# A hybrid transformer block on one core: filler matmuls at stage boundaries, weight tiles in rounds of two, and attention work moved

## The chip, the core and the metric

The kernel runs on one core of a Trainium2 chip. The core's engines have queues of their own and meet only at semaphores: TensorE (PE; its weight loads are shown as PEld), VectorE (DVE), ScalarE (ACT), GpSimd (POOL, hardly used here) and SyncE (SP), which issues the DMAs. The metric is the device time of one execution in microseconds (us).

## The reference

One layer: a half-step SwiGLU feed-forward layer, attention, and a second half-step feed-forward layer, on 256 tokens of 2048 features, in float32.

```python
f = swiglu(modulate(rms_norm(h, g_ffn1[l]), sh1, sc1), w1_gate[l], w1_up[l], w1_down[l])
h = h + 0.5 * gt1[:, None, :] * f
nrm = modulate(rms_norm(h, g_mix[l]), sh2, sc2)
q, k, v = jnp.split(nrm @ w_qkv[l], 3, axis=-1)      # 16 heads of 128
...
o_na = rms_norm(o_na.reshape(B, S, D_NA), g_out_na[l])     # heads 0 to 7
o_dil = rms_norm(o_dil.reshape(B, S, D_DIL), g_out_dil[l]) # heads 8 to 15
mix = jnp.concatenate([o_na, o_dil], axis=-1) @ w_o[l]
h = h + gt2[:, None, :] * mix
f = swiglu(modulate(rms_norm(h, g_ffn2[l]), sh3, sc3), w2_gate[l], w2_up[l], w2_down[l])
h = h + 0.5 * gt3[:, None, :] * f
```

The nine vectors `sh`, `sc` and `gt` come from `silu(c) @ w_ada + b_ada`, a product of one vector with a matrix of 2048 by 18432.

## The kernel before

Features lie on the partitions and the 256 tokens on the columns. All weights are streamed once, in tiles `rw` of 128 x 1024 (512 KB, eight blocks of 128 x 128). For precision each tile is split: ACT rounds it to `hiw` (L146), DVE subtracts to get the rest, `low` (L149). The activations are split in the same way and lie side by side, so that a block takes two matmuls: `hiw` times both halves (512 columns) and `low` times the upper half (256 columns). `hiw` and `low` have four buffers each, `rw` has five. Class `W` hands the tiles out in order: `prepare` issues and splits ahead, up to three tiles beyond the one in use (`AHEAD`); `add` collects eight blocks and then runs the eight `hiw` matmuls (L353) and the eight `low` matmuls (L355).

The adaLN vectors are 144 columns. Each is one DMA of 1 MB and one dot product of 2048 elements on DVE (L129), called a dot below. They are queued with `bg_add` and spread by a rate (`pace`): so many dots per weight tile. `bg_until` forces the rest at a point.

The program runs through these stages:

- the start: squares, the first norm, and six k-steps of the first layer done with unsplit weights (L514), each needing two dots;
- the first feed-forward layer: up (`pa`, `pb`), down (`pd`); its tiles are `w1_a` to `w1_e`;
- attention: 96 units of one tile project queries, keys and values in four groups of four heads (three times eight units a group, L637 and L640); 32 units of one tile are the output projection (`wo_unit`, L674 and L679), first over heads 0 to 7 (`b` = 0, units 96 to 111), then over heads 8 to 15 (`b` = 1, units 112 to 127). Between the units stand the steps of the heads, at units that `PLAN` and `PLAN_L` give as (a, b, c, d): transposes `pT`, scores, transposes `pP` of the softmax, and the product `po`;
- the second feed-forward layer, likewise, with tiles `w2_a` to `w2_e`.

At the end of a stage comes a norm over features. `Stat` squares each finished `h`, adds the squares on DVE (`sqa`), and sums them over the partitions with two matmuls with a matrix of ones (`pstat`, L208 and L209); `rstd_from` (L164) turns the sum into `rsr` with two ACT and four DVE instructions. Then `norm_pair` (L222, L223, L225) makes the next stage's `nx` two at a time; the first eight tiles of the next stage run while the later pairs are made.

The output norm of the attention is applied after the projection: `fin` (L654) copies the upper half of `pso` (ACT), adds the lower half, multiplies by the gate and the row `rsr`, and adds to `h` (DVE). So it waits for the sum over all eight heads of its half.

Order: tile dependencies are tracked by a framework that also orders each engine's queue. Where `manual_schedule` is open, or an instruction is pinned with `keep_in_program_order`, the order is that of the code: PE alone in units 8 to 120, PE, DVE and ACT (`BORDER`) from the last quarter of the first layer's down projection to unit 7, and again from unit 121 (`END - TAIL`) to the end of the second layer's first eight tiles. Elsewhere the framework chooses.

Of the kernel before, what the change touches and what calls it, by code (L numbers as in the profile page):

```python
# [9 lines left out]
F32 = mybir.dt.float32  # L10
# [27 lines left out]
PLAN_L = ((4, 6, 9, 11), (6, 8, 11, 13), (7, 9, 12, 14), (9, 11, 14, 15))  # L38
# [5 lines left out]
RQ = 0.35  # L44
# [3 lines left out]
WARM = 8  # L48
ARA = 2
# [17 lines left out]
def build(tc, a):  # L67
    nc = tc.nc
    with ExitStack() as ctx:
# [17 lines left out]
        def bank(nm):  # L87
            return pools["p"].tile([P, 512], F32, tag="b", name=nm)

# [86 lines left out]
        class Stat:  # L176
# [11 lines left out]
            def add(self, t, last_dve=True, late=False):  # L188
# [13 lines left out]
                elif n < total:  # L202
                    self.late = sq
                    if not late:
                        self.fold()
                else:
# [92 lines left out]
        class W:  # L299
            def __init__(self):  # L300
# [6 lines left out]
                self.credit = 0.0  # L307

# [9 lines left out]
            def prepare(self, ahead=AHEAD, pin=False):  # L318
# [11 lines left out]
            def chunk(self):  # L330
                self.prepare()
                self.tail += 1
                return self.ready.pop(self.tail - 1)

            def add(self, out, r, first, last, then=None, whole=False):
# [3 lines left out]
                self.todo.append((out, r, first, last, whole))  # L339
# [7 lines left out]
                for b, (out, r, first, last, whole) in enumerate(todo):  # L347
                    w = hi[:, b * P : (b + 1) * P]
                    if whole:
                        nc.tensor.matmul(out[:, :S], w, r[:, 0, :], start=first, stop=False)  # L350
                        nc.tensor.matmul(out[:, :S], w, r[:, 1, :], start=False, stop=False)
                    else:
                        nc.tensor.matmul(out, w, r, start=first, stop=False)  # L353
                for b, (out, r, first, last, whole) in enumerate(todo):
                    nc.tensor.matmul(out[:, :S], lo[:, b * P : (b + 1) * P], r[:, 0, :], start=False, stop=last)  # L355
# [22 lines left out]
        def up_mm(ps, k0, k1, first, last, then=None):  # L378
            for j in range(2):
                for k in range(k0, k1):  # L380
                    end = k == k1 - 1
                    ws.add(ps[:, j, :], nx[k], first and k == k0, last and end, then if end and j else None)
# [17 lines left out]
        def ffn_down(fs, hid, gate, stat=None, out=None, order=None):  # L400
            acc_ = {}
            for d, f in down_order(fs):
# [4 lines left out]
                if order is not None and d == KT - 4 and f == fs[0]:  # L407
                    order.enter_context(tc.manual_schedule(engines=BORDER))
# [3 lines left out]
                def update(d=d, whole=whole):  # L412
# [5 lines left out]
                    if stat is not None:  # L418
                        stat.add(h[d], late=d >= KT - 4)
# [518 lines left out]
```

## Time and profile before

| | |
|---|---|
| time, median of 3 (lowest to highest) | 1939.87 us (1939.45 to 1940.7) |
| the profiled execution | 1940.85 us |
| its span, first to last instruction | 1939.0 us |
| busy: PE, DVE, ACT | 1900.1, 1524.3, 902.8 us |
[...]
| moved by DMA | 503.98 MB, 260 GB/s |

Busy is the time in which an engine had at least one instruction under way. Matmuls overlap, so PE busy for 98% of the span says that PE rarely stood still, not that it ran at its best rate. Around the span lie 1.85 us of the execution in which no instruction is shown.

### The profile page before, as it was taken

The numbers are of one execution on the slowest core, as the hardware profiler recorded it, in microseconds if no ns is written. First come the engines' busy times: TensorE is split into PE (matmuls) and PEld (weight loads), VectorE is DVE, ScalarE is ACT, GpSimd is POOL, SyncE is SP. The second block draws the span as 40 slices with busy tenths as digits, with TensorE's granted clock in tenths as the row PEclk, the third lists the DMA queues.
The fourth block names the chain that finished last, engine by engine and source line by source line (L and its number), as shares of the span: only waits on it lengthen the run. The fifth ranks groups of instructions, "written<-read, shape, count | busy, mean of one in ns | idle before, by whom it ended". The sixth has DMA issues, their size and how long they took to land.

```text
span 1939.0 us, 27422 instructions
## 1 busy us (share of the span) xinstructions
PE 1900.1 (98%) x10528; PEld 1653.7 (85%) x10528; DVE 1524.3 (79%) x2058; ACT 902.8 (47%) x1327; POOL 0.7 (0%) x6
## 2 busy tenths in 40 slices
PE   8999999999999998999999997999999999999999
PEld 6888888888888887888788886888888888888888
DVE  7999999999788888799977897668865655545665
ACT  2545444433344454555555654544444433334442
POOL 0000000000000000000000000000000000000000
PEclk9999999999999999999999998999999999999999
DMA  9998888889988888589854453669866556656664
GB/s 400 404 362 310 312 309 302 312 330 408 343 308 341 314 312 292 199 329 323 321 192 163 153 157 105 198 213 321 321 206 186 189 189 187 193 187 188 190 194 134
DMA packets 120084, 503.98 MB, mean 260 GB/s; under 512 B 13329, under 2 KB 15633, under 8 KB 101521
## 3 DMA queue, kind: packets, MB, share of 16 engines
q1 hardware_dynamic: 119952, 502.24, 73.8%
q8 instruction: 82, 1.34, 0.3%
q14 instruction: 50, 0.40, 0.1%
HBM read 500.09 MB, written 2.10 MB: 259 GB/s over the span
## 4 chain that ended last, share of the span: by engine, by line
PE 90%; DVE 5%; DMA 2%; issue 1%; ACT 1%; SPq 0%; ACTq 0%; DVEq 0%
PE pb L353 29%; PE pd L353 16%; PE pb L355 15%; PE pd L355 8%; PE pqv L637 3%; PE pqk L637 3%; PE pqq L637 3%; PE pa L353 3%; PE pa L514 2%; DVE low L149 2%; PE pqv L640 2%; DMA ra<-in_w_ada_dram 2%; PE pa L355 1%; PE pqk L640 1%; PE pqq L640 1%
## 5 line engine op out<-in xcount | busy, mean ns | idle before, releaser
L146 ACT CAST hiw<-rw 128x1024 fp32r<-128x1024 f32 x644 | 674.0, 1050 | 784.5 <-PE pd L353 228.8
L149 DVE TENSOR_TENSOR low<-rw,hiw 128x1024 fp32r<-128x1024 f32 x644 | 782.7, 1221 | 302.7 <-ACT hiw L146 300.0
L353 PE MATMUL pb<-nx,hiw 128*128 128x512 f32 x2432 | 610.7, 393 | 4.1 <-DVE nx L225 4.1
L353 PEld LDWEIGHTS pb<-nx,hiw 128*128 128x128 f32 x2432 | 438.5, 189 | 83.3 <-issue 4.8
L355 PEld LDWEIGHTS pb<-nx,low 128*128 128x128 f32 x2432 | 332.3, 191 | 24.8 <-DVE low L149 1.2
L353 PE MATMUL pd<-hd,hiw 128*128 128x512 f32 x1384 | 346.7, 392 | 0.0
L355 PE MATMUL pb<-nx,low 128*128 128x256 f32 x2432 | 339.9, 283 | 0.5 <-DVE low L149 0.5
L353 PEld LDWEIGHTS pd<-hd,hiw 128*128 128x128 f32 x1384 | 248.9, 189 | 44.4
L129 DVE CUSTOM_DVE_ANT_0 ra<-ra,cb,vec 128x2048 f32<-128x2048 f32 x109 | 255.6, 2345 | 15.7 <-DMA ra<-in_w_ada_dram 15.3
L355 PEld LDWEIGHTS pd<-hd,low 128*128 128x128 f32 x1408 | 191.8, 190 | 14.0 <-DVE low L149 0.7
L355 PE MATMUL pd<-hd,low 128*128 128x256 f32 x1408 | 196.4, 282 | 0.3 <-DVE low L149 0.3
L417 DVE SCALAR_TENSOR_TENSOR h<-pd,m,h 128x256 f32<-128x256 f32 x126 | 59.4, 480 | 57.6 <-PE pd L355 57.2
L129 DVE CUSTOM_DVE_ANT_0 rx<-rx,cb,vec 128x2048 f32<-128x2048 f32 x35 | 82.1, 2345 | 3.7 <-DMA rx<-in_w_ada_dram 3.7
L353 PE MATMUL pa<-nx,hiw 128*128 128x512 f32 x288 | 72.3, 393 | 0.0
L637 PE MATMUL pqv<-hiw,nx 128*128 128x512 f32 x256 | 66.1, 401 | 3.5 <-ACT nx L223 3.5
L637 PE MATMUL pqk<-hiw,nx 128*128 128x512 f32 x256 | 65.0, 396 | 0.0
L637 PE MATMUL pqq<-hiw,nx 128*128 128x512 f32 x256 | 64.6, 394 | 0.0
L674 PE MATMUL pso<-ox,hiw 128*128 128x512 f32 x240 | 61.8, 401 | 0.0
L637 PEld LDWEIGHTS pqv<-hiw,nx 128*128 128x128 f32 x256 | 48.9, 194 | 13.9 <-ACT nx L223 3.9
L353 PEld LDWEIGHTS pa<-nx,hiw 128*128 128x128 f32 x288 | 51.9, 189 | 9.3
L637 PEld LDWEIGHTS pqq<-hiw,nx 128*128 128x128 f32 x256 | 46.8, 188 | 9.1
L637 PEld LDWEIGHTS pqk<-hiw,nx 128*128 128x128 f32 x256 | 46.5, 188 | 8.9
(145 smaller groups left out, 1380.9 us busy)
## 6 DMA issues: line engine op xcount, KB each, us to landing
ra<-in_w_ada_dram SPq DMA_DIRECT2D x109, 1024.0 KB, 7.3
rw<-in_w_b_dram SPq DMA_DIRECT2D x200, 512.0 KB, 4.4
rw<-in_w_d_dram SPq DMA_DIRECT2D x128, 512.0 KB, 4.3
rw<-in_w_c_dram SPq DMA_DIRECT2D x96, 512.0 KB, 3.6
rw<-in_w_qkv_dram SPq DMA_DIRECT2D x96, 512.0 KB, 4.7
rx<-in_w_ada_dram SPq DMA_DIRECT2D x35, 1024.0 KB, 7.5
rw<-in_w_e_dram SPq DMA_DIRECT2D x48, 512.0 KB, 4.1
rw<-in_w_a_dram SPq DMA_DIRECT2D x44, 512.0 KB, 6.8
```

Source lines behind the costliest of these rows:

```text
L129: dot = nc.vector.tensor_tensor_reduce(out=raw, in0=raw, in1=cb, scale=1.0, scalar=vec[:, BA + i : BA + i + 1], op0=ALU.mult, op1=ALU.add, ...
L146: cast = nc.scalar.copy(hi, raw)
L149: nc.vector.tensor_tensor(lo, raw, hi.bitcast(F32), ALU.subtract)
L353: nc.tensor.matmul(out, w, r, start=first, stop=False)
L355: nc.tensor.matmul(out[:, :S], lo[:, b * P : (b + 1) * P], r[:, 0, :], start=False, stop=last)
L417: nc.vector.scalar_tensor_tensor(h[d], part_, gate(d), h[d], ALU.mult, ALU.add)
L514: nc.tensor.matmul(pa[f][:, q, :], w[:, b * P : (b + 1) * P], full[k], start=k == 0 and q == 0, stop=k == K1 - 1 and q == 1, skip_group_ch ...
L637: nc.tensor.matmul(ps[t], nx[k][:, i, t * P : (t + 1) * P], whi[:, kk * 512 : (kk + 1) * 512], start=k + i == 0, stop=False)
L640: nc.tensor.matmul(ps[t], nx[k][:, 0, t * P : (t + 1) * P], wlo[:, kk * 512 : (kk + 1) * 512], start=False, stop=k == KT - 1)
L674: nc.tensor.matmul(ps, w, o, start=kk == 0, stop=False)
```

## The change

It has five parts.

1. `keep_warm(n)` issues n matmuls of 128 x 128 ones whose result nobody reads: 16 at the start between the sum of squares and the first k-step, and 4 ahead of and 13 behind the sum at the end of the first layer and of attention.
2. Class `W` gets `group`: with 2, `add` collects sixteen blocks and runs sixteen `hiw` matmuls, then sixteen `low` matmuls. With `turn` a round may begin with the `low` matmuls whose sums already exist, if the round before ended in `low`; then it ends with `hiw`. `group` is 2 in the first layer from its first down projection on, and in the second layer from its third pair of outputs on, where `turn` is on too; the last four `d` of a layer go back to 1. The weights of the second layer's up projections and of the last twelve of the first are laid out in half columns (`halves`) for it. `ahead` is one less for the last tiles of a layer, at the end of attention, and for the first tile of the stages that follow.
3. Heads 0 to 7 are normed before the projection: `d_ew` keeps `raw_o`, `total(0)` sums at unit 73, `normed_o` multiplies and splits at units 76 to 90. `fin` for `b` = 0 is then two DVE instructions on `h`.
4. The sum for heads 8 to 15 is one matmul, issued behind unit 113 (`total(1)`); it stood ahead of unit 112, as two. In the last seven units squares are taken one unit later (`sqs`). The last head's c step moves from unit 110 to 109 (a and b one unit too).
5. All 22 dots of attention are pinned, at a rate of 0.27 instead of 0.35 a tile, and the rest is forced at unit 95 instead of 115.

```diff
-PLAN_L = ((4, 6, 9, 11), (6, 8, 11, 13), (7, 9, 12, 14), (9, 11, 14, 15))
+PLAN_L = ((4, 6, 9, 11), (6, 8, 11, 13), (7, 9, 12, 14), (8, 10, 13, 15))
-RQ = 0.35
+RQ = 0.27
+WA = 4
+WB = 13
+        def keep_warm(n):
+
+            ps = bank("warm")
+            for i in range(n):
+                nc.tensor.matmul(ps[:, :P], ones, ones, start=True, stop=True)
...
+            def total_up(self):
+                self.ps = bank("pstat")[:, :S]
+                nc.tensor.matmul(self.ps, ones, self.acc, start=True, stop=True)
...
-                if len(self.todo) < 8:
+                if len(self.todo) < 8 * self.group:
                     return
-                hi, lo = self.chunk()
+                tiles = [self.chunk(self.ahead - i) for i in range(self.group)]
...
+                new = {t[5] for t in todo if t[2]}
+                early = [b for b, t in enumerate(todo) if t[5] not in new] if self.turn and self.ended_lo else []
+                late = [b for b in range(len(todo)) if b not in early]
...
+                for b in early:
+                    low(b, False)
...
+                for b in late:
+                    low(b, todo[b][3])
+                self.ended_lo = bool(late)
...
-                if order is not None and d == KT - 4 and f == fs[0]:
-                    order.enter_context(tc.manual_schedule(engines=BORDER))
+                if fs[-1] == FT - 1 and d == KT - 4 and f == fs[0]:
+                    ws.group, ws.turn = 1, False
+                    if order is not None:
+                        order.enter_context(tc.manual_schedule(engines=BORDER))
+                if stat is not None and d == KT - 1 and f == fs[4]:
+                    ws.ahead = AHEAD - 1
...
                     if stat is not None:
+                        if d == KT - 1:
+                            keep_warm(WA)
                         stat.add(h[d], late=d >= KT - 4)
+                        if d == KT - 1:
+                            keep_warm(WB)
...
+        with tc.manual_schedule(engines=STARTUP):
+            keep_warm(2 * WARM)
...
                 def fin(ps):
                     if b == 1:
                         hst.fold()
+                    gt2 = mods[5]
+                    if b == 0:
+                        for part_ in (ps[:, :S], ps[:, S:]):
+                            nc.vector.scalar_tensor_tensor(h[d], part_, gt2[:, d : d + 1], h[d], ALU.mult, ALU.add)
+                        return
...
-                    if b == 1:
-                        hst.add(h[d], late=u > END - TAIL)
+                    if u == END:
+                        keep_warm(WA)
+                        hst.add(h[d])
+                        keep_warm(WB)
+                    elif u >= END - TAIL:
+                        sqs.append(d)
+                    elif b == 1:
+                        hst.add(h[d])
...
+            def total(b):
+
+                ost[b].total_up()
+                if b == 0:
+                    rows[0] = ost[0].rstd(8 * HD)
+                    for hd in range(8):
+                        at(76 + 2 * hd, lambda hd=hd: normed_o(hd))
+
+            def normed_o(hd):
+                nc.vector.tensor_tensor(raw_o[hd], raw_o[hd], rows[0], ALU.mult)
+                split(raw_o[hd], ox[hd][:, 0, :], ox[hd][:, 1, :])
...
-            pinned.update(last[:ARA + 1])
+            pinned.update(last)
...
-                    if u == END - 2 * TAIL:
+                    if u == LAST - KT:
                         bg_until(0)
+                    ws.ahead = AHEAD - (u in (0, END))
...
+            ws.ahead = AHEAD if k else AHEAD - 1
         order.close()
         for f in range(NG):
             up_finish(f, ps2[f], {}, hid)
+        ws.group, ws.turn = 2, True
```

Three places show what this does to the queues. The first is DVE's where the norm of the queries of heads 4 to 7 is made (`rq` and `rqr` its factors, `qn` the normed queries, `ra` a dot's column, `low` a split). Before:

```order
L169 TENSOR_SCALAR rq_8475<-ss 128x8
L129 ISA ra_8644,m_85<-ra_8644,cb,vec 128x2048
L129 ISA m_85 128x1
L171 TENSOR_TENSOR rq_8474<-rqr 128x8
L149 TENSOR_TENSOR low<-rw,hiw 128x1024
L172 TENSOR_TENSOR rq_8474<-rq_8474,rq_8475 128x8
L149 TENSOR_TENSOR low<-rw,hiw 128x1024
L173 SCALAR_TENSOR_TENSOR rqr<-rq_8474,rqr 128x8
L136 SCALAR_TENSOR_TENSOR m_85<-m_85,vec 128x1
L129 ISA ra_8743,m_84<-ra_8743,cb,vec 128x2048
L129 ISA m_84 128x1
L605 SCALAR_TENSOR_TENSOR qn_8507<-pqq_8155,rqr,gq 128x128 x4
```

And now, at the same place:

```order
L177 TENSOR_SCALAR rq_8499<-ss 128x8
L179 TENSOR_TENSOR rq_8498<-rqr 128x8
L180 TENSOR_TENSOR rq_8498<-rq_8498,rq_8499 128x8
L181 SCALAR_TENSOR_TENSOR rqr<-rq_8498,rqr 128x8
L656 SCALAR_TENSOR_TENSOR qn_8528<-pqq_8183,rqr,gq 128x128 x2
L157 TENSOR_TENSOR low<-rw,hiw 128x1024
```

Two dots and two splits that stood between the first factor and the first normed query are gone from there.

The second place is DVE's queue where the factor `rsr` of heads 8 to 15 is made and the first `fin` of `b` = 1 follow (`wt` their scratch tile, `h_90` the output). Before:

```order
L169 TENSOR_SCALAR rs_10652<-pstat 128x256
L665 TENSOR_TENSOR h_93<-h_93,wt 128x256
L171 TENSOR_TENSOR rs_10651<-rsr 128x256
L172 TENSOR_TENSOR rs_10651<-rs_10651,rs_10652 128x256
L173 SCALAR_TENSOR_TENSOR rsr<-rs_10651,rsr 128x256
L149 TENSOR_TENSOR low<-rw,hiw 128x1024
L663 TENSOR_TENSOR wt<-wt,pso 128x256
L664 SCALAR_TENSOR_TENSOR wt<-wt,m_83,rsr 128x256
L665 TENSOR_TENSOR h_90<-h_90,wt 128x256
```

And now:

```order
L157 TENSOR_TENSOR low<-rw,hiw 128x1024 x2
L177 TENSOR_SCALAR rs_10663<-pstat 128x256
L179 TENSOR_TENSOR rs_10662<-rsr 128x256
L721 TENSOR_TENSOR wt<-wt,pso 128x256
L180 TENSOR_TENSOR rs_10662<-rs_10662,rs_10663 128x256
L181 SCALAR_TENSOR_TENSOR rsr<-rs_10662,rsr 128x256
L724 SCALAR_TENSOR_TENSOR wt<-wt,m_83,rsr 128x256
L721 TENSOR_TENSOR wt<-wt,pso 128x256
L725 TENSOR_TENSOR h_90<-h_90,wt 128x256
L724 SCALAR_TENSOR_TENSOR wt<-wt,m_83,rsr 128x256
L157 TENSOR_TENSOR low<-rw,hiw 128x1024
L725 TENSOR_TENSOR h_90<-h_90,wt 128x256
```

The two splits ahead of it are those of the tiles of units 116 and 117, and behind the factor two units' `fin` stand together.

The third place is ACT's queue in the last units of the output projection (`hiw` the rounding of a coming tile, `wt` the copy out of `pso`, `sq` the square of a finished `h`). Before:

```order
L195 ACTIVATE sq<-h_92 128x256
L146 CAST hiw<-rw 128x1024
L662 COPY wt<-pso 128x256
L195 ACTIVATE sq<-h_92 128x256
L146 CAST hiw<-rw 128x1024
L662 COPY wt<-pso 128x256
```

And now:

```order
L154 CAST hiw<-rw 128x1024
L717 COPY wt<-pso 128x256
L203 ACTIVATE sq<-h_92 128x256
L154 CAST hiw<-rw 128x1024
L717 COPY wt<-pso 128x256
L203 ACTIVATE sq<-h_92 128x256
```

The square that stood between one unit's `h` and the next tile's rounding is now behind the next unit's copy.

## Rows read from the trace of the kernel before

**Rows 1.** the table of stretches, here the first feed-forward layer (columns: the stretch in us, its length, then busy us and instruction count in brackets of PE, PEld, DVE, ACT and POOL, the granted clock as a share of 2.4 GHz, the DMA share and GB/s).

```profile
62.00:775.00 713.00, 707.23 (x4053) 621.04 (x4051) 654.42 (x807) 328.62 (x414) 0.00 (x0) 1.00 0.89 329
```

**Rows 2.** the waits of PE over the whole program (engine and line that waited, `<-` who was waited for: us in total, times, longest us).

```profile
PE pstat L208 <- DVE sqa L185: 11.7, 2, 10.2
PE pT L694 <- DVE qn L620: 2.0, 1, 2.0
PE pT L694 <- DVE qn L605: 1.7, 2, 1.0
PE pstat L209 <- ACT sq L195: 1.3, 1, 1.3
PE pP L732 <- DVE sc L726: 1.3, 2, 1.0
PE po L155 <- DVE pl L159: 1.2, 1, 1.2
```

**Rows 3.** the same table of stretches for two that lie behind pauses of PE.

```profile
774.04:780.86 6.82, 5.78 (x14) 4.58 (x15) 6.09 (x15) 3.49 (x8) 0.00 (x0) 0.50 0.57 220
1183.64:1200.70 17.06, 7.23 (x18) 5.08 (x19) 13.92 (x28) 6.39 (x14) 0.00 (x0) 0.50 0.30 93
```

**Rows 4.** the order in time on PE in the second feed-forward layer (start us, length us, engine, line, operation, output <- inputs, columns and count; a piece lasts until the end of its last matmul, so a run's share of PE's time is the next piece's start less its own).

```profile
1212.12 2.00 PE L353 MATMUL pb<-nx,hiw 128*128 128x512 f32 x8
1213.96 1.11 PE L355 MATMUL pb<-nx,low 128*128 128x256 f32 x8
...
1217.71 2.00 PE L353 MATMUL pb<-nx,hiw 128*128 128x512 f32 x8
```

**Rows 5.** the same view on PE in the query, key and value projection, where matmuls of `low` have 512 columns too.

```profile
805.11 1.98 PE L637 MATMUL pqk<-hiw,nx 128*128 128x512 f32 x8
806.92 1.07 PE L640 MATMUL pqk<-low,nx 128*128 128x512 f32 x4
```

**Rows 6.** the order in time around the end of the first feed-forward layer, engines mixed (same columns; in square brackets idle time before the piece and who ended it).

```profile
767.48 1.12 PE L355 MATMUL pd<-hd,low 128*128 128x256 f32 x8
768.40 1.22 DVE L149 TENSOR_TENSOR low<-rw,hiw 128x1024 fp32r<-128x1024 f32 x1 [1.48 <-ACT hiw L146]
769.88 0.48 DVE L417 SCALAR_TENSOR_TENSOR h<-pd,m,h 128x256 f32<-128x256 f32 x1
770.87 0.70 PE L209 MATMUL pstat<-sq,ones 128*128 128x256 f32 x2
773.54 0.43 DVE L173 SCALAR_TENSOR_TENSOR rsr<-rs,rsr 128x256 f32<-128x256 f32 x1
775.08 3.78 PE L637 MATMUL pqv<-hiw,nx 128*128 128x512 f32 x8 [3.51 <-ACT nx L223]
```

**Rows 7.** the same view at the end of the eight units that norm and project at once.

```profile
793.73 0.87 DVE L222 SCALAR_TENSOR_TENSOR nt<-h,m,rsr 128x256 f32<-128x256 f32 x2
794.24 0.91 ACT L223 ACTIVATE nx<-nt,m 128x256 fp32r<-128x256 f32 x2 [1.69 <-DVE nt L222]
796.95 1.98 PE L637 MATMUL pqv<-hiw,nx 128*128 128x512 f32 x8
```

**Rows 8.** the same view where the key and query tiles of head group 1 are made.

```profile
931.86 2.35 DVE L129 CUSTOM_DVE_ANT_0 ra<-ra,cb,vec 128x2048 f32<-128x2048 f32 x1
934.53 0.33 PE L694 MATMUL pT<-ident,qn 128*128 128x128 f32 x1 [1.01 <-DVE qn L605]
```

**Rows 9.** the same view between the two halves of the output projection.

```profile
1132.59 1.22 PE L209 MATMUL pstat<-sq,ones 128*128 128x256 f32 x2 [1.32 <-ACT sq L195]
1133.25 3.40 PE L674 MATMUL pso<-ox,hiw 128*128 128x512 f32 x8
1136.49 1.10 PE L679 MATMUL pso<-ox,low 128*128 128x256 f32 x8
...
1148.47 1.99 PE L674 MATMUL pso<-ox,hiw 128*128 128x512 f32 x8
1148.91 1.22 DVE L149 TENSOR_TENSOR low<-rw,hiw 128x1024 fp32r<-128x1024 f32 x1
1151.24 1.08 PE L674 MATMUL pso<-ox,hiw 128*128 128x512 f32 x4
1151.69 1.22 DVE L149 TENSOR_TENSOR low<-rw,hiw 128x1024 fp32r<-128x1024 f32 x1
```

**Rows 10.** the same view around the end of the output projection and the start of the second feed-forward layer.

```profile
1178.01 1.10 PE L679 MATMUL pso<-ox,low 128*128 128x256 f32 x8
1182.35 0.42 ACT L195 ACTIVATE sq<-h 128x256 f32<-128x256 f32 x1 [2.73 <-DVE h L665]
1189.61 0.42 DVE L665 TENSOR_TENSOR h<-h,wt 128x256 f32<-128x256 f32 x1
1190.54 1.22 PE L209 MATMUL pstat<-sq,ones 128*128 128x256 f32 x2
1195.88 3.75 PE L353 MATMUL pb<-nx,hiw 128*128 128x512 f32 x8 [4.12 <-DVE nx L225]
```

**Rows 11.** the same view at the end of that start.

```profile
1214.44 0.91 ACT L223 ACTIVATE nx<-nt,m 128x256 fp32r<-128x256 f32 x2 [1.69 <-DVE nt L222]
```

**Rows 12.** the order in time at the program's start.

```profile
55.25 0.51 ACT L235 ACTIVATE xf<-nt,m 128x256 f32<-128x256 f32 x1 [6.44 <-DVE nt L233]
19.40 42.94 PE L514 MATMUL pa<-xf,rw 128*128 128x256 f32 x189 [6.98 <-ACT xf L235]
```

More of the change, by code (lines that the diff above doesn't have):

```diff
@@ L205, in add @@
                         self.fold()
+                elif not last_dve:
+                    nc.vector.tensor_tensor(self.acc, self.acc, sq, ALU.add)
                 else:
@@ L307, in __init__ @@
                 self.credit = 0.0
+                self.ahead = AHEAD
+                self.group = 1
+                self.turn = False
+                self.ended_lo = False
             def fetch(self, n):
@@ L328, in prepare, with chunk, add @@
                             bg_use()
-            def chunk(self):
-                self.prepare()
+            def chunk(self, ahead=None):
+                self.prepare(ahead)
                 self.tail += 1
                 return self.ready.pop(self.tail - 1)
-            def add(self, out, r, first, last, then=None, whole=False):
-                self.todo.append((out, r, first, last, whole))
+            def add(self, out, r, first, last, then=None, whole=False, key=None):
+                self.todo.append((out, r, first, last, whole, key))
@@ new lines, in add, with weights, low @@
+                early = [b for b, t in enumerate(todo) if t[5] not in new] if self.turn and self.ended_lo else []
+                late = [b for b in range(len(todo)) if b not in early]
+                def weights(b, half):
+                    return tiles[b // 8][half][:, b % 8 * P : (b % 8 + 1) * P]
+                def low(b, stop):
+                    out, r = todo[b][:2]
+                    nc.tensor.matmul(out[:, :S], weights(b, 1), r[:, 0, :], start=False, stop=stop)
+                for b in early:
+                    low(b, False)
@@ L349, in add @@
+                for b, (out, r, first, last, whole, key) in enumerate(todo):
+                    w = weights(b, 0)
+                    stop = last and b in early
                     if whole:
                         nc.tensor.matmul(out[:, :S], w, r[:, 0, :], start=first, stop=False)
-                        nc.tensor.matmul(out[:, :S], w, r[:, 1, :], start=False, stop=False)
+                        nc.tensor.matmul(out[:, :S], w, r[:, 1, :], start=False, stop=stop)
                     else:
-                        nc.tensor.matmul(out, w, r, start=first, stop=False)
@@ L354, in add @@
-                for b, (out, r, first, last, whole) in enumerate(todo):
-                    nc.tensor.matmul(out[:, :S], lo[:, b * P : (b + 1) * P], r[:, 0, :], start=False, stop=last)
+                        nc.tensor.matmul(out, w, r, start=first, stop=stop)
+                for b in late:
+                    low(b, todo[b][3])
+                self.ended_lo = bool(late)
                 for then in thens:
@@ L378, in up_mm @@
         def up_mm(ps, k0, k1, first, last, then=None):
[L379 to L382, printed above, removed]
+            step = 8 if k1 - k0 == KT else k1 - k0
+            for ka in range(k0, k1, step):
+                for j in range(2):
+                    for k in range(ka, ka + step):
+                        end = k == k1 - 1
+                        ws.add(ps[:, j, :], nx[k], first and k == k0, last and end, then if end and j else None,
+                               key=(id(ps), j))
         def up_finish(f, ps, part, hid):
@@ L466, in build @@
         with tc.manual_schedule(engines=STARTUP):
-            warm = bank("warm")
-            for i in range(WARM):
-                nc.tensor.matmul(warm[:, :P], ones, ones, start=True, stop=True)
+            keep_warm(WARM)
             pc = []
@@ L575, in na_bias @@
                 return t
-            ox = [ac.tile([P, 2, S], F32R, tag=f"ox{i}", name=f"ox{i}") for i in range(NH)]
+            ox = [ac.tile([P, 2, S], F32R, tag=f"ox{i}", name=f"ox{i}") for i in range(12)]
+            raw_o = [ac.tile([P, 2, S], F32, tag=f"ox{i}", name=f"ro{i}") for i in range(12, NH)]
+            raw_o = [raw_o[i // 2][:, i % 2, :] for i in range(8)]
             ost = [Stat(8), Stat(8)]
```

36 lines of the change are left out of this document (25 added, 11 removed).

## Prediction

> **What bounds the kernel now.** I read the stage table first. In the first feed-forward layer PE is busy for 707.23 of 713.00 us and DVE for 654.42, which is 92% [rows 1]: PE sets the pace, with DVE close behind it. Whatever shortens PE's queue shortens the program, as long as DVE, ACT and the loads follow. So I looked for the times in which PE does not run at its best: its waits [rows 2], the stretches at half the granted clock [rows 3], and the cost of a single matmul when nothing is in the way [rows 4, 5]. The waits add up to little, with one exception: 11.7 us for the sum of squares, 10.2 of it in one piece at the end of attention. The reader should see that the change touches these places one by one, and hardly the 1,900 us in between.
>
> All gains below are taken from the profiled execution: 1940.85 us, of which 1939.0 are its span and 1.85 lie around it. The median of the runs is 0.98 lower, and I take that off at the end.
>
> **Rounds of two tiles.** PE's work is the same, but it changes less often from `low` runs (256 columns) to `hiw` runs (512 columns). Counted in the two orders, such changes fall from 514 to 267 over both feed-forward layers: 65 fewer in the first, 182 fewer in the second (there `turn` removes one and a half per round of two). Eight `hiw` matmuls behind a `low` run take 1213.96 - 1212.12 = 1.84 us [rows 4]. Where the matmuls ahead of them had 512 columns too, eight take 806.92 - 805.11 = 1.81 [rows 5]. The `low` run that follows starts about 0.01 sooner for it, so I count 0.02 per change: 247 x 0.02 = **4.9 us**. Bounds: 0, if the 0.03 is only the modelling of ends, and 247 x 0.03 = 7.4.
>
> [...]
>
> **End of the first layer.** Before, DVE runs a split at 768.40 for 1.22 us while the last `pd` sums finish (the `low` run began at 767.48 and lasts 1.12, to 768.60); so the last `h` starts only at 769.88 [rows 6]. With `ahead` one less that split is no longer there, and `h` can start at about 768.7: 1.15 us earlier. The sum (770.87, two matmuls in 0.70) runs at full clock if the fillers hold it, which gives about 0.1 more on the path. The first projection matmul thus comes 1.25 us sooner. A filler has 128 columns; as half of one matmul of the sum, 0.70 / 4 = 0.18 us [rows 6], four of them take an estimated 0.7 and thirteen 2.3 us, and both fit into waits: PE waits 3.51 us ahead of 775.08. I cost them at nothing; without that cover they would cost up to 3.
>
> With the clock held, the stretch 774.04 to 780.86, granted at 0.50 [rows 3], runs at 1.00. Its 5.78 us of busy PE would take half of that, 2.6 to 2.9 less. But then PE meets the chain that makes `nx`. The last pair is ready at 794.24 + 0.46 (half of 0.91) - 775.08 = 19.6 us after the first projection matmul, and PE goes on to the ninth unit at 796.95 - 775.08 = 21.9 [rows 6, 7]. The split that was dropped has to be made in these eight units, so I put the last pair 1.15 later, at 20.8. Of the clock's 2.6 only 1.1 remains. Sum: 1.25 + 1.1 = **2.4 us**, bounds 1.2 (all given back) and 3.9 (no norm chain in the way).
>
> **Waits in attention.** PE waited 2.0 + 1.7 us for `qn` and 1.3 for `sc` [rows 2]. At head group 1 the last dot runs from 931.86 for 2.35 us, to 934.21, and `pT` can start at 934.53 [rows 8]: the dot stands in DVE's queue ahead of the queries. In the new order two dots and two splits are gone from between the factor and the first `qn`. I take all three waits as gone: **5.0 us**, bounds 2.5 (half of it moves to another group) and 5.9 (some shorter waits go too).
>
> **Middle of the output projection.** Heads 0 to 7 are normed before their projection, so their sum is made at unit 73. The pair of `pstat` ahead of unit 112 goes with its wait: 1.3 for the square, 1133.25 - 1132.59 = 0.66 for the pair, and the slow run behind it, 1136.49 - 1133.25 = 3.24 against 1.84, so 1.4 [rows 2, 4, 9]. The wait of `po` for `pl`, 1.2 [rows 2], goes with the last head's steps one tile earlier. Together 4.6, less some 0.3 for the two single sums that stand elsewhere now: **4.3 us**, bounds 2.0 and 4.6.
>
> **End of attention.** This is the large place. The last `low` run ends at 1178.01 + 1.10 = 1179.1, the sum's last matmul starts at 1190.54 and the first of the second layer at 1195.88 [rows 10]: 16.8 us, 11.4 up to the sum and 5.3 behind it. In the last units ACT squares `h`, waits 2.73 for it, and only then rounds the next tile; DVE waits for that rounding. By the new order the square stands behind the next unit's copy, and that ring is broken. But the sum for heads 8 to 15 is made behind unit 113 now, and its `rsr` comes 773.54 + 0.43 - 770.87 = 3.1 us behind the sum, by the case in [rows 6]. The `fin` of units 112 to 115 queue up there. I count four units at 2.78 us of DVE (1148.91 to 1151.69 [rows 9]) less one split (1.22), two square adds and one add (0.42 each): 8.6 us. So `h` of unit 115 is done 3.1 + 8.6 - 2 x 2.77 = 6.2 us behind PE's end of that unit. PE takes 1151.24 - 1148.47 = 2.77 a unit and DVE 2.78, so DVE does not catch up; only the last units, with no tile left to split, give back 1.1. The last `h` is then 5.1 behind PE, the sum at 5.5 and the first `pb` at 5.5 + 5.3 = 10.8 instead of 16.8: 6.0 us. Behind that the clock (0.50 up to 1200.70 [rows 3]) is again worth 2.4 and again meets the norm chain: the last pair is ready at 1214.44 + 0.46 - 1195.88 = 19.0 [rows 10, 11], plus 1.15 is 20.2, against 1217.71 - 1195.88 = 21.8 before [rows 4]: 1.6. Sum **7.6 us**. Bounds: -1 (the backlog takes all that the broken ring gives, and the four fillers ahead of the sum stand on the path) and 12 (no backlog, full clock).
>
> **The rest.** Sixteen fillers at the start cost nothing: the k-steps wait for dots. The last `xf` is made at 55.25 to 55.76, and PE ends its k-steps at 19.40 + 42.94 = 62.3, having waited 6.98 for `xf` [rows 12]. Rounds ask for two tiles at once, and the last units release work in bursts; I set 0.6 us of new short waits against the rest.
>
> Sum: 4.9 + 2.4 + 5.0 + 4.3 + 7.6 - 0.6 = 23.6. So 1940.85 - 23.6 = 1917.25 for a profiled execution, and 1917.25 - 0.98 = **1916.3 us** for the median.
>
> **Rivals.**
> (a) The rounds give nothing: the difference of 0.03 is in the record and not in the array. [...] Against it: the same size shows in any neighbouring pair of runs. Time: 1916.3 + 4.9 = 1921.2.
> (b) DVE does catch up at the end of attention. For it: 2.78 against 2.77 leaves all to small savings, and the new `fin` of `b` = 0 leaves work out. Against it: PE's units are no longer stretched by waits. The first `pb` comes about 4 us sooner: 1912.3.
> (c) The fillers do not hold the clock, or the waits in attention move instead of vanishing. The clock's 1.1 + 1.6 go and half of the 5.0: 1916.3 + 2.7 = 1919.0, or + 2.5 = 1918.8, or both, 1921.5. Against it: the new order spaces the dots evenly.
> (d) Slower. `hiw` and `low` have four buffers each, exactly two rounds of two. A round holds two until its end, so ACT and DVE refill in twos, with DVE 92% busy [rows 1]. There are 65 + 121 = 186 rounds. If each waits 23.6 / 186 = 0.13 us, everything is given back; from there it is slower. At 0.2 us a round the time is 1916.3 + 37 = 1953.5. Against it: PE now shows no such wait among its longest [rows 2], and a round also gives twice the time to refill.
> (e) The change moves waits only, and all of them come back at the next stage: within 0.2%, 1939.
>
> **Chances.** The forecast 0.54, (a) 0.13, (b) 0.12, (c) 0.11, (d) 0.05, (e) 0.05. About 0.2%, 3.9 us, is what a measurement of this kernel can tell from no change. The forecast and (a) to (c) are all faster by more: 0.90. (e) is 0.05 the same, (d) 0.05 slower. The range reaches 1908 (b, with both clock terms whole and the rounds at 0.03) and 1924 (a and c together, nearly), and leaves out (d), (e) and little else.
>
> **What would show it.** In the profile after: no stretch at 0.50 around the two boundaries; eight `hiw` matmuls inside a round of sixteen about 0.02 to 0.03 shorter than the first eight; no wait of `pT` for `qn` over 1 us; first `pb` of the second layer 10 to 11 us behind the last `pso`; ninth projection unit about 20.8 behind the first. The forecast falls if PE shows a wait for `hiw` or `low` in every round, or if the first `pb` comes 15 us or more behind.

## The result and the profile after

The changed kernel takes 1917.59 us (median of 4 runs, 1915.61 to 1918.86) against 1940.19 (4 runs, 1939.45 to 1940.7): ratio 0.9881, 95% interval 0.9867 to 0.9896. The profiled execution took 1916.35, span 1914.6, so it gained 24.5 us on the one of before. The line of busy time on its page hardly differs; what changed is how little of PE's time is wait or half clock (the mean granted clock is 0.998, against 0.991 in the profile of before):

```profile
PE 1898.3 (99%) x10624; PEld 1660.2 (87%) x10624; DVE 1522.3 (80%) x2052; ACT 902.3 (47%) x1319; POOL 0.7 (0%) x6
```

To see where the gain came from, I took from both traces the start of the same matmul (the first of a stage, or the first `hiw` matmul of an attention unit) and its difference, after less before:

| place | difference, us | gained since the row above |
|---|---|---|
| first `pb` of the first layer | +0.24 | -0.24 |
| last `low` run of the first layer | -0.66 | 0.90 |
| attention, unit 0 | -1.93 | 1.27 |
| unit 2 | -4.61 | 2.68 |
| unit 8 | -2.79 | -1.82 |
| unit 62 | -6.58 | 3.79 |
| unit 77 | -2.93 | -3.65 |
| unit 111 | -5.14 | 2.21 |
| unit 117 | -9.79 | 4.65 |
| first `pb` of the second layer | -19.87 | 10.08 |
| its fifth tile | -22.07 | 2.20 |
| its ninth tile | -20.83 | -1.24 |
| PE's last matmul | -24.47 | 3.64 |

The waits of PE after, the counterpart of [rows 2] (same columns):

```profile
PE pT L772 <- DVE qn L671: 2.2, 1, 2.2
PE pb L388 <- DVE nx L239: 1.9, 3, 1.2
PE pqv L688 <- ACT nx L237: 1.5, 3, 0.6
PE pP L810 <- DVE sc L804: 1.5, 1, 1.5
PE pstat L219 <- DVE sq L201: 0.6, 1, 0.6
```

The 11.7 us for `sqa` are gone. [rows 2] leaves out three rows of its view, each longer than any shown but the first: 7.0 us for `xf` at the start, 4.1 and 3.5 for `nx` ahead of the first matmul behind either boundary; they stand in the brackets of [rows 6, 10, 12]. So waits for `nx` are not new: they were 7.6 us in two pieces and are 3.4 in six, some of them at later tiles. New is one long wait each for `qn` and `sc` at other units than before. The stretches for [rows 1, 3] (columns as there) show the granted clock at 1.00 behind both pauses (1.00 is the profile's full rate; no run here shows it in GHz):

```profile
62.00:775.00 713.00, 711.59 (x4096) 626.94 (x4095) 656.12 (x811) 329.54 (x415) 0.00 (x0) 1.00 0.89 329
773.15:778.70 5.55, 5.55 (x24) 4.59 (x25) 5.01 (x12) 2.70 (x7) 0.00 (x0) 1.00 0.49 195
1176.01:1181.60 5.59, 5.59 (x32) 4.91 (x33) 5.05 (x13) 3.01 (x7) 0.00 (x0) 1.00 0.00 0
```

The end of attention in order of time answers to [rows 9, 10]: first the end of units 119 and 122 on PE with three splits and the `h` of these units on DVE, then the pause:

```profile
1146.03 1.11 PE L745 MATMUL pso<-ox,low 128*128 128x256 f32 x8
1147.40 1.22 DVE L157 TENSOR_TENSOR low<-rw,hiw 128x1024 fp32r<-128x1024 f32 x1
1149.65 0.49 DVE L724 SCALAR_TENSOR_TENSOR wt<-wt,m,rsr 128x256 f32<-128x256 f32 x1
1150.09 1.23 DVE L157 TENSOR_TENSOR low<-rw,hiw 128x1024 fp32r<-128x1024 f32 x1
1151.57 0.42 DVE L725 TENSOR_TENSOR h<-h,wt 128x256 f32<-128x256 f32 x1
1154.32 1.07 PE L745 MATMUL pso<-ox,low 128*128 128x256 f32 x8
1155.71 1.22 DVE L157 TENSOR_TENSOR low<-rw,hiw 128x1024 fp32r<-128x1024 f32 x1
1157.81 0.43 DVE L725 TENSOR_TENSOR h<-h,wt 128x256 f32<-128x256 f32 x1
...
1168.22 1.10 PE L745 MATMUL pso<-ox,low 128*128 128x256 f32 x8
1169.16 1.05 PE L96 MATMUL warm<-ones 128*128 128x128 f32 x8
1170.31 0.42 DVE L725 TENSOR_TENSOR h<-h,wt 128x256 f32<-128x256 f32 x1
1171.25 0.70 PE L219 MATMUL pstat<-sq,ones 128*128 128x256 f32 x2 [0.55 <-DVE sq L201]
1171.79 3.06 PE L96 MATMUL warm<-ones 128*128 128x128 f32 x26
1176.01 2.08 PE L388 MATMUL pb<-nx,hiw 128*128 128x512 f32 x8 [1.16 <-DVE nx L239]
```

From the end of attention on PE (1169.32) to the first `pb` it is 6.7 us; before it was 16.8. The last `h` is done 1.4 us behind PE; it was 4.85 at unit 119 (1151.99 against 1147.14) and 2.85 at unit 122 (1158.24 against 1155.39). Behind `wt` (1149.65) DVE now runs a split; in the kernel before, at a unit like those of [rows 9], it ran the `h` that needs this `wt`:

```profile
1150.83 0.48 DVE L664 SCALAR_TENSOR_TENSOR wt<-wt,m,rsr 128x256 f32<-128x256 f32 x1
1151.35 0.42 DVE L665 TENSOR_TENSOR h<-h,wt 128x256 f32<-128x256 f32 x1
```

The new wait for `qn`, at unit 77, and what stands ahead of it on DVE:

```profile
1000.31 2.34 DVE L137 CUSTOM_DVE_ANT_0 ra<-ra,cb,vec 128x2048 f32<-128x2048 f32 x1
1002.99 0.34 DVE L656 SCALAR_TENSOR_TENSOR qn<-pqq,rqr,gq 128x128 f32<-128x128 f32 x1
1008.89 0.28 DVE L671 TENSOR_TENSOR qn<-ra,rb 128x128 f32<-128x128 f32 x1
1009.22 0.33 PE L772 MATMUL pT<-ident,qn 128*128 128x128 f32 x1 [2.25 <-DVE qn L671]
```

It is [rows 8] again at another head group: a dot among the queries, and PE late by about its length.

### The profile page after: what moved, and what is told of

Its sections match the earlier page's. It is cut to its first block, busy times and chain, and to the rows that moved or that the text cites. A ratio compares the mean times of both kernels' runs of the same rounds, so it can differ in the third digit from the quotient of the medians.

```text
span 1914.6 us, 27571 instructions
## 1 busy us (share of the span) xinstructions
PE 1898.3 (99%) x10624; PEld 1660.2 (87%) x10624; DVE 1522.3 (80%) x2052; ACT 902.3 (47%) x1319; POOL 0.7 (0%) x6
## 3 DMA queue, kind: packets, MB, share of 16 engines
q8 instruction: 83, 1.36, 0.3%
## 4 chain that ended last, share of the span: by engine, by line
PE 88%; DVE 9%; ACT 1%; issue 1%; DMA 1%; DVEq 0%; SPq 0%; ACTq 0%
PE pb L388 26%; PE pd L388 15%; PE pb L377 14%; PE pd L377 8%; PE pqk L688 3%; PE pso L740 3%; PE pa L388 3%; DVE low L157 3%; PE pqq L688 2%; PE pa L562 2%; PE pqv L688 2%; DVE ra L137 2%; PE pqk L691 2%; PE pso L745 2%; PE pa L377 1%
## 5 line engine op out<-in xcount | busy, mean ns | idle before, releaser
L388 PE MATMUL pb<-nx,hiw 128*128 128x512 f32 x2432 | 581.1, 391 | 1.9 <-DVE nx L239 1.9
L388 PEld LDWEIGHTS pb<-nx,hiw 128*128 128x128 f32 x2432 | 446.7, 188 | 88.7 <-issue 1.3
L388 PE MATMUL pd<-hd,hiw 128*128 128x512 f32 x1384 | 328.5, 390 | 0.0
L377 PEld LDWEIGHTS pb<-nx,low 128*128 128x128 f32 x2432 | 311.9, 191 | 13.1 <-DVE low L157 1.2
L377 PE MATMUL pb<-nx,low 128*128 128x256 f32 x2432 | 316.0, 283 | 0.5 <-DVE low L157 0.5
L388 PEld LDWEIGHTS pd<-hd,hiw 128*128 128x128 f32 x1384 | 255.0, 188 | 49.8
L377 PEld LDWEIGHTS pd<-hd,low 128*128 128x128 f32 x1408 | 179.1, 191 | 6.8 <-DVE low L157 1.0
L377 PE MATMUL pd<-hd,low 128*128 128x256 f32 x1408 | 181.6, 283 | 0.4 <-DVE low L157 0.3
L429 ACT COPY gu<-pb 128x512 f32<-128x512 f32 x56 | 32.9, 587 | 52.4 <-PE pb L388 29.5
```

Of the source, the lines that this page charges most:

```text
L377: nc.tensor.matmul(out[:, :S], weights(b, 1), r[:, 0, :], start=False, stop=stop)
L388: nc.tensor.matmul(out, w, r, start=first, stop=stop)
L429: nc.scalar.copy(t, ps[:, :, :S])
```

## Experiments

Where nothing else is said, each is the changed kernel with one edit. "Later" and "earlier" compare its profile with that of the changed kernel at the same matmul. Ratios are to the kernel before; their intervals are about 0.0015 to each side, so a place in the trace says more than a median here.

**Rounds of one tile.**

```diff
-            ws.group = 2
+            ws.group = 1
-        ws.group, ws.turn = 2, True
+        ws.group, ws.turn = 1, False
```

> The changed kernel with rounds of one tile everywhere (group 1, turn off), the half-column layout kept. Theory: the second feed-forward layer loses the steady 0.06 us per four tiles that its trace shows against before (-20.83 us at its seventeenth tile-half, -24.47 at the end, so 3.6 us), and the first layer its 0.9: together 4.5 us, all of it in those stages and none at a boundary; about 1922 us. Rival: the 0.06 comes from something else than the order of the runs (the layout, the loads), and the time stays within 1 us of 1917.6.

1920.46 us, ratio 0.9893 (0.9878 to 0.9907); the profile is 4.23 us longer, 0.40 of it in the first layer and 3.63 from the second layer's first `pb` on, in even steps. Four tiles, first with rounds of two, then with rounds of one (two kernels, same view):

```profile
1262.72 7.44 PE L388 MATMUL pb<-nx,hiw 128*128 128x512 f32 x32
1270.00 4.00 PE L377 MATMUL pb<-nx,low 128*128 128x256 f32 x32
1273.84 7.44 PE L388 MATMUL pb<-nx,hiw 128*128 128x512 f32 x32
```

```profile
1256.12 2.00 PE L388 MATMUL pb<-nx,hiw 128*128 128x512 f32 x8
1257.96 1.11 PE L377 MATMUL pb<-nx,low 128*128 128x256 f32 x8
...
1267.30 2.00 PE L388 MATMUL pb<-nx,hiw 128*128 128x512 f32 x8
```

1273.84 - 1262.72 = 11.12 against 1267.30 - 1256.12 = 11.18: 0.06 for three changes fewer, 0.02 each. The theory holds in the second layer; in the first it gives 0.4 instead of 0.9.

**No unread matmuls at the two boundaries.** (`WA = 0`, `WB = 0`; nothing that is read is left out.)

> The changed kernel without the 4 and 13 unread matmuls at the end of the first layer and of attention (the 16 at the start stay). Theory: the granted clock falls to 0.50 in both pauses again, the first two tiles behind each cost 2.7 and 2.2 us more, and the waits for the norm pairs that the trace of the changed kernel shows behind (1.65 and 1.0 us) go in turn; with the sums at half clock 2 to 3 us more in all, about 1920. Rival 1: the pauses are now short enough (6 to 7 us without the fillers) that the clock stays at 1.00 without them: within 0.5 us. Rival 2: the norm chain sets the time of these tiles alone, and the fillers give nothing even if the clock falls: within 0.7 us.

1918.07 us, ratio 0.9883; the profile is 1.36 us longer. The clock does fall, at the first boundary to 0.50 (774.50 to 776.00). The first two tiles of the second layer, by stretches:

```profile
1176.00:1178.00 2.00, 1.57 (x4) 1.31 (x5) 1.82 (x5) 1.05 (x3) 0.00 (x0) 0.50 0.03 8
1178.00:1180.00 2.00, 2.00 (x7) 1.53 (x6) 1.82 (x6) 0.93 (x3) 0.00 (x0) 0.51 0.00 0
1180.00:1182.00 2.00, 2.00 (x14) 1.82 (x13) 1.82 (x5) 1.17 (x3) 0.00 (x0) 1.00 0.00 0
```

At the first boundary unit 1 is 1.57 us later, and at unit 8 all of it is given back, since PE hardly waits for `nx` there any more (its one wait is the 3.5 us ahead of the first matmul; in the changed kernel units 6 and 7 wait 0.49 each). At the second, 1.62 us are lost by the second tile and 0.4 remain at the ninth. Another 0.55 come 130 us later, where PE waits for `low` behind a dot that waited 2.11 us for its load; the same place costs time in other profiles too (see the dots at named units). So rival 2 is right: the clock falls, and costs 0 and 0.4 us.

**The square in the same unit again.**

```diff
-                        sqs.append(d)
+                        hst.add(h[d], late=u > END - TAIL)
```

> The changed kernel with the square of a finished h in the same unit again in the last units (as before), all else of the change kept. Theory: this ring (square waits for h, the rounding of the next tile waits behind it on ACT, the split behind that on DVE) was most of the pause at the end of attention: units of DVE at 4.3 us against 2.77 of PE come back, the first product of the second layer lies 13 to 16 us behind PE's last of attention instead of 6.9, and the time is 6 to 9 us longer, 1924 to 1927. Rival: the pause got shorter by what else is left out there (one split less, the sums placed elsewhere), and the ring counts less than 3 us: under 1920.6.

1926.62 us, ratio 0.9923 (0.9907 to 0.994); the profile is 9.75 us longer, 8.37 of it between unit 127 and the first `pb`. The ring is back on ACT and DVE, and PE waits for `sqa`:

```profile
1169.04 0.42 ACT L203 ACTIVATE sq<-h 128x256 f32<-128x256 f32 x1 [2.73 <-DVE h L725]
1169.37 1.03 ACT L154 CAST hiw<-rw 128x1024 fp32r<-128x1024 f32 x1
1170.43 1.22 DVE L157 TENSOR_TENSOR low<-rw,hiw 128x1024 fp32r<-128x1024 f32 x1 [1.48 <-ACT hiw L154]
1173.39 0.42 ACT L203 ACTIVATE sq<-h 128x256 f32<-128x256 f32 x1 [2.73 <-DVE h L725]
1178.30 1.19 PE L218 MATMUL pstat<-sqa,ones 128*128 128x256 f32 x2 [7.66 <-DVE sqa L193]
```

One unit takes 1173.39 - 1169.04 = 4.35 us. The theory holds: the ring was most of that pause.

**The old dots.** (Rate 0.35, three pinned, the rest forced at the old unit.)

> The changed kernel with the 22 dots of attention as before: rate 0.35, three pinned, the rest forced at the old unit. Theory: the waits for qn and sc are made by dots that stand ahead of them on DVE. Then the waits at units 70 and 77 of the changed kernel (1.6 and 2.5 us) go or shrink, and those of before at units 42, 53 and 101 (1.2, 2.2, 2.2) come back: 1918 to 1920. Rival: the two new waits come from the sum for heads 0 to 7 that the change puts at unit 73 and stay; with the old ones on top the time is 5 us or more above 1917.6.

1914.17 us, ratio 0.9859 (0.9844 to 0.9874): below the changed kernel, though the intervals overlap. The waits at units 70 and 77 are gone (1.65 and 2.35 us earlier), and 3.35 us come at units 35 to 42; those of before at 53 and 101 do not come back. So neither expectation holds for these, and by profile the even spacing of the dots costs 0.7 us of attention. The new wait has another cause than the old ones:

```profile
881.14 2.35 DVE L137 CUSTOM_DVE_ANT_0 ra<-ra,cb,vec 128x2048 f32<-128x2048 f32 x1 [1.37 <-DMA ra<-in_w_ada_dram]
...
884.62 0.61 DVE L804 TENSOR_SCALAR sc<-sc,sm 128x256 f32<-128x256 f32 x2
```

The dot stands at the head of DVE's queue and waits for its own load; the softmax behind it waits too, and PE for that.

**The even dots in the kernel before.** (Rate 0.27, all pinned, the rest forced at unit 95; nothing else of the change.)

> The kernel before with its 22 dots of attention as in the change: rate 0.27, all pinned, the rest forced at unit 95. With the old dots in the changed kernel the waits of before at units 53 and 101 did not come back. Theory: either alone removes them, since each takes some DVE work from ahead of the queries; here the waits at 42, 53, 62 and 101 (1.2, 2.2, 0.5, 2.2 us) go and one at 70 or 77 comes, because a dot lies in units 67 and 74 here too: 2 to 4 us less than before, about 1937. Rival: the waits at 53 and 101 are set by other work (the norm of heads 0 to 7, the lighter output of the first half) and stay; the time is within 2 us of before.

1940.28 us (10 runs), ratio 1.0003 (0.9994 to 1.0013). In the profile the waits at units 42, 53 and 62 go (1.20, 2.15, 0.54 us), and at 70 and 77 come 2.70 and 1.88: from unit 2 to unit 77 it is 0.69 us slower than before, the same as in the changed kernel. The wait at unit 101 stays, as the rival had it for that one. So the theory is right on which of the other waits go and come, but both new ones come, and the time is the rival's. It is the other edits that remove the wait at 101; which of them was not tried.

This profile (1938.06 us) is 2.8 us shorter than that of the kernel before, and the spacing is not why. Up to unit 2 and again in units 111 and 112 the order on PE, DVE and ACT is the same in both, and 1.2 and 1.5 us less go by; the mean granted clock is 0.992 here and 0.991 there. Ahead of unit 112 PE waits 1.32 us as in [rows 9], but the run behind that wait takes 2.19 us instead of 3.40, where the clock was 0.50 (1132.44 to 1135.85):

```profile
1131.48 0.70 PE L209 MATMUL pstat<-sq,ones 128*128 128x256 f32 x2 [1.32 <-ACT sq L195]
1131.83 2.19 PE L674 MATMUL pso<-ox,hiw 128*128 128x512 f32 x8
```

So the time that these two places take differs from one execution to the next, with the order unchanged; that the 1.2 us up to unit 2 are the clock too was not shown.

**Dots at named units.** (`DOT_UNITS` says at which units the rate is 1, otherwise 0; none in units 63 to 70 and 72 to 78.)

> The changed kernel with the 22 dots of attention at named units: none in units 63 to 70 and 72 to 78, otherwise at least three units apart. Theory: a dot (2.3 us) in units 67 and 74 stands ahead of the softmax of head 11 and of the queries of heads 8 to 11, and makes the waits at units 70 and 77 (1.65 and 2.47 us with what follows); with none there both are gone, 4 us less, about 1913.6, and no wait of the rate 0.35 (unit 38, a dot that itself waits for its load) comes. Rival: the wait at 77 is made by the factor of heads 0 to 7 (four DVE instructions, 1.7 us, at the same units) and stays over 1.2 us; then 2 us less or nothing.

1914.45 us, ratio 0.9865 (0.985 to 0.988). From unit 0 to unit 77 it gains 3.47 us, both waits are gone. 1.2 us are given back at unit 94, and 2.1 in the second layer, where in this execution a dot came late:

```profile
1308.12 2.35 DVE L138 CUSTOM_DVE_ANT_0 ra<-ra,cb,vec 128x2048 f32<-128x2048 f32 x1 [2.49 <-DMA ra<-in_w_ada_dram]
...
1323.59 2.35 DVE L138 CUSTOM_DVE_ANT_0 ra<-ra,cb,vec 128x2048 f32<-128x2048 f32 x1 [1.28 <-DMA ra<-in_w_ada_dram]
1327.74 1.22 PE L378 MATMUL pb<-nx,low 128*128 128x256 f32 x8 [1.90 <-DVE low L158]
```

DVE's order there is that of the changed kernel. The theory holds for the dots of attention, and its rival falls: the factor of heads 0 to 7 is still made at these units.

**Late dots pinned.** (The 16 dots of the second layer pinned at one per ten tiles.)

> The changed kernel with the 16 dots of the second feed-forward layer pinned at one per ten tiles, and nothing else. Theory: the 2.5 us between its executions (1915.6 and 1916.4 against 1918.8 and 1918.9) are waits behind such dots; they all come out near the lower two, 1915 to 1917, within 1.5 us of each other. Rival: the scatter lies elsewhere (the start, the first layer): it stays, and the median is within 1 us of 1917.6.

1917.45 us (1916.23 to 1919.04), ratio 0.9886. The scatter stays: the rival is right. In this profile 1.0 us is lost ahead of the first `pb`, and from there on nothing differs by more than 0.1. The theory has a part in it all the same: six profiles with these dots as in the changed kernel lose 0.4 to 2.2 us at the place shown above, and the two with the late dots pinned lose nothing there.

**One tile less ahead for the first five tiles.**

```diff
-                    ws.ahead = AHEAD - (u in (0, END))
+                    ws.ahead = AHEAD - (u < 5 or u == END)
-            ws.ahead = AHEAD if k else AHEAD - 1
+            ws.ahead = AHEAD if k > 8 else AHEAD - 1
```

> The changed kernel with one tile less split ahead for the first five tiles of attention and of the second feed-forward layer (three again from the sixth tile on). Theory: behind each boundary the norm pairs on DVE are what PE waits for (units 6 and 7 of attention 1.3 us, unit 5 0.3; 1.0 us at two tiles of the second layer), because two splits stand ahead of the fourth pair. One split of 1.18 us less ahead of it: 1.2 us less at the first boundary, 1.0 at the second, 2.2 in all, about 1915.4. Rival: tiles then come too late, PE waits for hiw or low in these tiles, and nothing or less than 0.5 us is won.

1918.3 us, ratio 0.9886. Unit 8 is 0.2 us later, not 1.2 earlier; the second layer gains 0.3. The rival is right: PE now waits for the tile instead of the norm.

```profile
790.21 2.11 PE L688 MATMUL pqv<-hiw,nx 128*128 128x512 f32 x8 [0.52 <-ACT hiw L154]
793.74 2.11 PE L688 MATMUL pqv<-hiw,nx 128*128 128x512 f32 x8 [0.51 <-ACT hiw L154]
```

ACT rounds these tiles between the same norm steps, so a tile that is put off is late itself. This profile also shows something else, 1.6 us at unit 77: the wait for `qn` is the same 2.25 us as in the changed kernel, but here the clock fell behind it:

```profile
1009.20:1012.90 3.70, 3.70 (x11) 2.92 (x11) 3.12 (x7) 1.13 (x2) 0.00 (x0) 0.56 0.85 258
```

In the changed kernel that stretch is at 1.00:

```profile
1009.30:1012.00 2.70, 2.70 (x13) 2.26 (x14) 2.70 (x6) 1.28 (x3) 0.00 (x0) 1.00 0.73 205
```

**The same without the unread matmuls.**

> One tile less ahead at both boundaries, and no unread matmuls there. Without the fillers alone, the time at unit 8 was the same as with them: the tiles at half clock lost 1.57 us and the norm chain gave all of it back. Theory: fillers and norm chain are two limits of one stretch; with the chain 1.2 us shorter the half clock is felt. Against the kernel with the shorter chain this one is then 1.2 us later at unit 8 and 1.5 to 2.2 us later in the second layer, 3 us in all, about 1918.5. Rival: the clock costs nothing there at all, and the two kernels stand within 0.7 us.

1920.61 us, ratio 0.9902. Against the kernel with one tile less ahead it loses 0.7 us up to unit 8 and 0.6 by the ninth tile of the second layer (another 0.36 behind the late dots): the clock, 0.61 from 772.60 to 780.00 and 0.77 from 1177.90 to 1185.00, is felt, at less than half of what the theory gave.

**Three tiles ahead everywhere.**

> The changed kernel with three tiles split ahead everywhere, as before, so that a split stands ahead of the last h of the first layer and of attention again. The prediction's step: the first projection comes 1.15 us later. Theory now: the split that is not made ahead has to be made in the eight tiles behind, where the norm chain on DVE is the limit, so that at unit 8 nothing is won or lost by it (within 0.3 us), and the same in the second layer: time within 0.8 us of the changed kernel. Rival: the 1.15 us stay at both places, 2 us longer, about 1919.8.

1917.01 us, ratio 0.9885. The first projection comes 1.27 us later, as the prediction's step had it, and unit 8 only 0.1; at the second boundary 1.0, of which nothing is left at the ninth tile (0.6 come later, behind the late dots). The theory holds: what is not split ahead has to be split behind.

**Two versions meant to be faster.** The first is the dots at named units with one tile less ahead; the second has no dot at unit 93, less ahead in the second layer only, and the late dots pinned.

> Both edits, one tile less ahead at the two boundaries and the dots at named units. They lie at different places, so the gains add: 6.2 us less than the changed kernel, about 1911.4. Rival: what is saved at unit 8 is waited for later in attention, and the sum is under 5 us.

> The changed kernel with the dots of attention at named units as in the run before, but without the one at unit 93 (it made 1.2 us of wait), one tile less ahead for the first tiles of the second feed-forward layer (0.3 us there in the run of the shorter chain), and the 16 dots of the second layer pinned at one per ten tiles, where the framework had put them two or three tiles apart. Theory: these dots wait for their loads and hold up DVE, by up to 2.5 us in one profile, which PE feels (2.1 us) in some executions and not in others; apart, they do not. Then the attention gains 4 us against the changed kernel, the second layer 0.3, and the scatter goes: 1911 to 1913, all runs within 1.5 us of each other. Rival: the scatter has another cause and stays at 2 to 3 us, the median at 1913 to 1915.

1914.54 us, ratio 0.9865 (0.985 to 0.9879), and 1913.83 us (1912.18 to 1914.73), ratio 0.9866 (0.9852 to 0.9881). Both rivals have the number: the gains are 1.5 and 2.5 us by profile, and the scatter stays (2.6 us in the second). The reason of the first does not hold, since nothing was saved at unit 8 that could be waited for later. The wait at unit 94 is there without its dot, at 0.8 instead of 1.2 us. The four versions without the wait at unit 77 lie at 0.9859 to 0.9866; the changed kernel and four that keep it (no unread matmuls, late dots pinned, one tile less ahead, three tiles ahead) at 0.9881 to 0.9886. That they are faster is likely; the intervals still overlap.

## Why the prediction came out, step by step

Predicted were 1916.3 us and 23.6 us of gain; measured are 1917.59 and, by profile, 24.5. The sum is right within 1 us, but two of its terms are off by more than that, in opposite directions. Of its signs, two did not come: `pT` waited 2.25 us for `qn`, and the first `pb` lay 6.7 behind the last `pso` instead of 10 to 11.

- **Rounds** (4.9): 4.0 measured, 3.63 of 3.64 in the second layer. The two samples of [rows 4, 5] stood for all. In the first layer 0.4 of 1.3 came out; there DVE is 92% busy [rows 1], but what takes the rest was not tried. Rival (a) falls: the same matmuls in another order take 0.02 us less per change (11.12 us against 11.18 for four tiles, three changes).
- **End of the first layer** (2.4): 2.13 from the last `low` run to unit 8. The first projection was to come 1.25 sooner, and came 1.27; the last norm pair was to hold PE until 20.8 us behind it, and unit 7 started at 794.00 - 773.15 = 20.85. (The prediction calls it the ninth unit; it is the eighth.) But the two parts are no sum. Without the fillers nothing is lost at unit 8, without the shorter `ahead` 0.1: either alone brings nearly all, because both meet the same norm chain. No run leaves out both. The fillers were read too short: a filler, like a matmul of the sum, is two records in the trace, so four are the x8 (1.05 us) and thirteen the x26 (3.06) where 0.7 and 2.3 were put. They still fit: PE waits 0.55 and 1.16 us behind them.
- **Attention waits** (5.0, bounds 2.5 to 5.9): 2.35 from unit 8 to unit 111, below the lower bound. The failed step is "I take all three waits as gone". The order was read at one head group; at the third, whose queries and keys take four more DVE instructions, the same change of spacing puts a dot among them. 1.65 and 2.47 us came new at units 70 and 77. By the two runs with dots exchanged, the even spacing itself costs 0.7 us, in the kernel before and after alike. This is the second half of rival (c), the waits that move instead of vanishing, priced at 2.5 us.
- **Middle** (4.3): 4.65, the edits there not tried one by one. About 1.5 of it is the slow run behind the wait ahead of unit 112 (3.40 us at 0.50), which another execution with the same order did not have (2.19 us, the even dots in the kernel before); nor did that one lose 1.2 of the 2.13 at the end of the first layer.
- **End of attention** (6.0 and 1.6): 10.08 and 0.96. The ring was most of it, 8.37 us by experiment. The failed step is "PE takes 2.77 a unit and DVE 2.78, so DVE does not catch up": of a backlog of 6.2 us, 5.1 were to be left at the end, and 1.4 were. It was 5.35 at unit 115 to begin with (`h` done at 1141.46, PE at 1136.11). Up to unit 119 it fell by 0.5: DVE took 1150.09 - 1147.40 = 2.69 a unit, PE 2.77 and 2.74 in turn. The 2.78 of [rows 9] has no wait in it either, but it is the length of the same five instructions in another order, with `h` directly behind the `wt` that it needs: it starts 0.04 us after the end of `wt`, where the split of the new order starts 0.05 before it. Then 2.0 more went at the change to the hand-written order, where DVE finishes three `h` between the splits at 1150.09 and 1155.71, and 1.4 in the last units. Rival (b), priced at 4 us and given 0.12, is what happened there: the first `pb` came 4.1 us sooner than forecast.
- **The rest** (-0.6): start and first layer together gave 0.66, rounds included. Among the profiles of the changed kernel and its variants the first `pb` starts between 163.19 and 164.82, so 1.6 us of scatter lie ahead of it.

Rival (d) fell: no wait comes with the rounds. The time lies near the forecast because the 3.4 us that the end of attention gave more and the 2.65 that the attention waits gave less nearly cancel; that is luck. The range, which took in both, was the honest part.

## What to carry to other kernels

The length of a unit's work, read in one order of a queue, need not hold in another: follow a backlog unit by unit, and through every place where the order changes, before saying that an engine can't catch up. Two edits that end at the same later limit are alternatives and not a sum; follow each to the first unit behind that limit. When work is spread evenly over a queue that runs in order, look at every place where a chain passes, not at one, and ask whether its own load has arrived.

## What the runs showed of the hardware

At unit 77 PE waited 2.25 us for `qn` in the changed kernel and with one tile less ahead, and 2.2 us with rounds of one. Behind it the granted clock was 1.00 in the changed kernel (1009.30 to 1012.00) and with rounds of one (1009.60 to 1012.40), and 0.56 with one tile less ahead (1009.20 to 1012.90), where the order on PE is that of the changed kernel: eight `hiw` matmuls took 3.07 us there instead of 1.91, and the four of `low` behind them 1.35 instead of 0.90, 1.6 us more together. Behind the wait of 1.32 us ahead of unit 112 the clock was 0.50 in the profile of the kernel before (1132.44 to 1135.85), and eight `hiw` matmuls lasted 3.40 us; in that of the same kernel with even dots, where the order is the same, they lasted 2.19 behind an equal wait, and 1.5 us less went by in units 111 and 112. And four tiles in the second layer took 11.12 us in rounds of two and 11.18 in rounds of one: 0.02 us for each of three changes from `low` runs (256 columns) to `hiw` runs (512). Over the 182 changes of that layer it was 3.63 us.
